# Three Pool transfers instead of one for the first row of a softmax

## The chip, the cores and the metric

The kernel runs on one core of one Trainium2 chip. The metric is the device time of one execution in microseconds (us), of which the profile's span, from the first to the last instruction, is all but about 2 us. A ratio of two kernels is the mean time of the one's fast runs over that of the other's in the same rounds on the same chip, so it is not quite the ratio of the medians quoted beside it; its 95% interval is given in brackets.

## The reference

```python
x = np.random.randn(32, 512, 1024).astype(np.float32); temperature = 0.5

def reference(x, temperature):
    scaled = x / temperature
    shifted = scaled - np.max(scaled, axis=-1, keepdims=True)
    exp_x = np.exp(shifted)
    return (exp_x / np.sum(exp_x, axis=-1, keepdims=True)).astype(np.float32)
```

That is a softmax over 16,384 rows of 1,024 numbers. Each byte is read once and written once: 67 MB in and 67 MB out.

## The kernel before

The rows are taken in 16 passes. A pass is a tile of 128 partitions by 8 rows (4 MB). SyncE loads it, VectorE takes maxima, ScalarE the exponentials with their sums, VectorE divides in place, and ScalarE issues the store. There are six tile buffers, so the seventh load waits for the stores of the first tile. Passes 0, 1, 14 and 15 are worked in two halves of four rows.

```python
ROWS = 8
BUFS = 6
PASSES = [[4, 4]] * 2 + [[8]] * 12 + [[4, 4]] * 2
...
    def load():
        i = len(tiles)
        if i < len(PASSES):
            xt = data.tile([P, ROWS, d], f32, name="xt")
            nc.sync.dma_start(out=xt, in_=dram(xf, i))
            tiles.append(xt)
...
    def store(g):
        i, a, k = groups[g]
        if g == 0:
            nc.gpsimd.dma_start(out=dram(of, i)[:, :1, :], in_=tiles[i][:, :1, :])
        elif a + k == ROWS:
            a = 1 if i == 0 else 0
            nc.scalar.dma_start(out=dram(of, i)[:, a:, :], in_=tiles[i][:, a:, :])
            load()
```

Only the very first row of each partition (128 x 4 KB, 0.5 MB) is stored by Pool, early, while ScalarE is still at work on the second half of the tile.

## Time and profile before

| | before |
|---|---|
| time, median of 6 runs | 317.71 us (317.35 to 317.98) |
| VectorE, ScalarE busy | 79%, 47% of the span |
| loads, ScalarE's stores | 49.7% and 48.9% of the 16 DMA engines |
| Pool's store | 0.4% of the 16 DMA engines |

The lines of the page stand in the prediction below: q1 are the loads, q10 ScalarE's stores, q0 Pool's store and q14 the fetching of instructions. The prediction also says how the trace's packets are strung into 16 chains, one for each DMA engine; "refill engines" are the two whose chains hold the q14 packets. In the kernel before, every chain comes out with exactly 128 load packets, 120 + 8 store packets and, but for one packet swapped between two chains, 8 packets of Pool's row, which is a check on the stringing. "A chain ends at 314.49" below always means this.

### The profile page before, as it was taken

The numbers are of one execution on the slowest core, as the hardware profiler recorded it, in microseconds if no ns is written. First come the engines' busy times: TensorE is split into PE (matmuls) and PEld (weight loads), VectorE is DVE, ScalarE is ACT, GpSimd is POOL, SyncE is SP. The second block draws the span as 40 slices with busy tenths as digits, with TensorE's granted clock in tenths as the row PEclk, the third lists the DMA queues.
The fourth block names the chain that finished last, engine by engine and source line by source line (L and its number), as shares of the span: only waits on it lengthen the run. The fifth ranks groups of instructions, "written<-read, shape, count | busy, mean of one in ns | idle before, by whom it ended". The sixth has DMA issues, their size and how long they took to land. (4 is left out here: it accounts for less than half of the span.)

```text
span 315.7 us, 534 instructions
## 1 busy us (share of the span) xinstructions
DVE 251.0 (79%) x146; ACT 148.1 (47%) x257; POOL 1.3 (0%) x5
## 2 busy tenths in 40 slices
DVE  0399999999679795897949979399793999979710
ACT  0176637680906519074290833808247091564700
POOL 0001000000000000000000000000000000000000
DMA  8999999999999999999999999999999999999996
GB/s 328 415 448 421 369 441 434 465 400 461 404 457 407 457 411 457 428 436 436 428 448 415 448 415 449 411 465 403 461 403 461 403 461 403 461 403 461 407 457 274
DMA packets 4755, 134.24 MB, mean 425 GB/s; under 512 B 528, under 2 KB 528, under 8 KB 656
## 3 DMA queue, kind: packets, MB, share of 16 engines
q1 hardware_dynamic: 2304, 67.11, 49.7%
q10 hardware_dynamic: 2304, 66.59, 48.9%
q0 software_dynamic: 144, 0.52, 0.4%
q14 instruction: 3, 0.02, 0.0%
HBM read 67.11 MB, written 67.11 MB: 425 GB/s over the span
## 5 line engine op out<-in xcount | busy, mean ns | idle before, releaser
L77 ACT ACTIVATE xt<-xt,bias 128x1024 f32<-128x1024 f32 x128 | 145.2, 1135 | 136.6 <-DVE bias L71 127.1
L68 DVE TENSOR_REDUCE top<-xt 128x8 f32<-128x8192 f32 (+1 forms) x20 | 139.5, 6976 | 44.4 <-DMA xt<-in_x_dram 44.4
L95 DVE TENSOR_SCALAR xt<-xt,recip 128x1024 f32<-128x1024 f32 x80 | 54.3, 748 | 0.5
L92 DVE TENSOR_TENSOR xt<-xt,recip 128x8192 f32<-128x8192 f32 x6 | 52.2, 8692 | 0.2
L77 ACT ACTIVATION_READ_ACCUMULATOR xt<-xt,bias 128x1 f32 x128 | 23.9, 187 | 0.0
L77 ACT ACT_TABLE_LOAD x1 | 1.3, 1283 | 13.3 <-DMA xt<-in_x_dram 13.3
L89 DVE RECIPROCAL recip<-sums 128x8 f32<-128x8 f32 (+1 forms) x20 | 3.8, 188 | 4.1 <-ACT xt L77 4.1
L71 DVE TENSOR_SCALAR bias<-top 128x8 f32<-128x8 f32 (+1 forms) x20 | 3.4, 171 | 0.7
L104 POOL DMA_DIRECT2D out_dram<-xt x1 | 1.1, 1142 | 23.4 <-DVE xt L95 23.4
L143 POOL MEMSET const-bfloat16-1.0<- 128x1 bf16 x1 | 0.1, 96 | 0.0
L143 POOL MEMSET const-float32-0.0<- 128x1 f32 x1 | 0.1, 93 | 0.2 <-issue 0.2
L143 POOL MEMSET const-float32-1.0<- 128x1 f32 x1 | 0.1, 93 | 0.0
L143 POOL MEMSET const-uint8-127<- 128x1 uint8 x1 | 0.1, 93 | 0.0
## 6 DMA issues: line engine op xcount, KB each, us to landing
xt<-in_x_dram SPq DMA_DIRECT2D x16, 4096.0 KB, 51.2
out_dram<-xt ACTq DMA_DIRECT2D x15, 4096.0 KB, 28.0
out_dram<-xt ACTq DMA_DIRECT2D x1, 3584.0 KB, 23.2
out_dram<-xt POOLq DMA_DIRECT2D x1, 512.0 KB, 19.6
```

The costliest lines, as they stand in the source:

```text
L68: nc.vector.tensor_reduce(out=top, in_=tiles[i][:, a : a + k, :], axis=mybir.AxisListType.X, op=extreme)
L71: nc.vector.tensor_scalar_mul(bias, in0=top, scalar1=-scale)
L77: nc.scalar.activation(tiles[i][:, a + b, :], tiles[i][:, a + b, :], mybir.ActivationFunctionType.Exp, bias=bias[:, b : b + 1], scale=scal ...
L89: nc.vector.reciprocal(recip, sums)
L92: nc.vector.tensor_mul(xt, xt, recip.unsqueeze(2).to_broadcast([P, k, d]))
L95: nc.vector.tensor_scalar_mul(tiles[i][:, a + b, :], in0=tiles[i][:, a + b, :], scalar1=recip[:, b : b + 1])
L104: nc.gpsimd.dma_start(out=dram(of, i)[:, :1, :], in_=tiles[i][:, :1, :])
L143: nc = _bacc.Bacc("TRN2", target_bir_lowering=False, num_devices=1)
```

## The change

Pool's row is still stored from all 128 partitions, but in parts of 4, 108 and 16.

```diff
+PARTS = (0, 4, 112, 128)
...
         if g == 0:
-            nc.gpsimd.dma_start(out=dram(of, i)[:, :1, :], in_=tiles[i][:, :1, :])
+
+            for p, q in zip(PARTS, PARTS[1:]):
+                nc.gpsimd.dma_start(out=dram(of, i)[p:q, :1, :], in_=tiles[i][p:q, :1, :])
```

## The prediction

What the sum needs is this assumption: the first transfer gives one row to each of 4 engines, the second 9 to each of the other 12, the third one to each of all 16. Then four engines carry 1 + 1 = 2 rows and twelve 9 + 1 = 10, where all had 8. The sum came to 317.8 - 0.5 = 317.3 us, or 317.4 with the rivals; its term of 0.5 us rests on these shares. The shares of the second rival (9, 8 and 4 rows) were assumed as well. The numbers of engines (0 to 15), here and in the expectations, follow the order in which the author took the transfers to fill the engines; no view names an engine.

> **What bounds the kernel now.** I read the page first (parts 1 and 2), then its DMA queues and issues, then the waits of the load queue, and last the DMA view of a short stretch at the end.
>
> ```profile
> DVE 251.0 (79%) x146; ACT 148.1 (47%) x257; POOL 1.3 (0%) x5
> ...
> DMA  8999999999999999999999999999999999999996
> ...
> q1 hardware_dynamic: 2304, 67.11, 49.7%
> q10 hardware_dynamic: 2304, 66.59, 48.9%
> q0 software_dynamic: 144, 0.52, 0.4%
> q14 instruction: 3, 0.02, 0.0%
> ...
> L104 POOL DMA_DIRECT2D out_dram<-xt x1 | 1.1, 1142 | 23.4 <-DVE xt L95 23.4
> ...
> xt<-in_x_dram SPq DMA_DIRECT2D x16, 4096.0 KB, 51.2
> out_dram<-xt ACTq DMA_DIRECT2D x15, 4096.0 KB, 28.0
> out_dram<-xt ACTq DMA_DIRECT2D x1, 3584.0 KB, 23.2
> out_dram<-xt POOLq DMA_DIRECT2D x1, 512.0 KB, 19.6
> ```
>
> No compute engine is near full: VectorE has 79%. The DMA row is 9 in every slice but the first and the last, and the loads (q1) and ScalarE's stores (q10) hold 98.6% of 16 engines' span. So the kernel is bound by the 16 DMA engines: 134 MB in 315.7 us. The changed transfer is queue q0: 0.4% of the DMA time. That alone caps what the change can do in a steady way at about 0.4% of 315.7 us, 1.3 us, unless it creates a wait.
>
> Could it create one? The sixth buffer's successor, the seventh load, reuses the first tile, so it must wait for that tile's stores.
>
> ```profile
> SPq L59 <- DMA out_dram<-xt: 214.3, 10, 42.9
> ```
>
> The load queue waits for stores all the time and it costs nothing, because loads already issued keep the engines fed. In the timeline Pool issues at 23.8 us, so its transfer lands at 23.8 + 19.6 = 43.4; ScalarE's store of the same tile issues at 32.9 and lands at 32.9 + 23.2 = 56.1. The seventh load is released by the second one, 12.7 us after Pool's.
>
> The trace keeps a start, a queue, a size and a duration for each DMA packet. Each starts within some nanoseconds of the end of another, so they string into 16 chains, one for each DMA engine. A 32,768-byte packet takes 1.213 us, a 28,672-byte one 1.062, a 4,096-byte one of Pool's store 0.159. One engine's share is 248 of the first (300.8), 8 of the second (8.5) and 8 of the third (1.3): 310.6 us, and the chains run without a gap worth naming from 1.8 us to 313.2 or later. The span ends 1.2 us after the last chain. So what ends the kernel is not the mean engine but the last one, and the DMA view of 311.8 to 313.8 us, in slices of 0.05 us, shows that they don't end together (each packet stands in the slice in which it starts):
>
> ```profile
> DMA  0009999909900090000000900000090000000000
> GB/s 0 0 0 655 2621 1966 1311 655 0 1311 655 0 0 0 655 0 0 0 0 0 0 0 655 0 0 0 0 0 0 656 0 0 0 0 0 0 0 0 0 0
> ```
>
> 655 GB/s in one slice is one 32 KB packet. Fourteen engines start their last data packet between 311.95 and 312.55; two stragglers start theirs at 312.9 and 313.28, and end at 314.12 and 314.49, when the mean of the other fourteen ends is 313.40 and the latest 313.73. Following these two chains back, they are the ones with the three instruction packets of q14: one has the packet at 84.5 us (0.31 us, and the load packet behind it 0.53 longer than usual: 0.84), the other the two at 65.2 and 190.4 (0.31 + 0.25 and 0.31 + 0.34: 1.2). So the two engines that refill instructions end last, by about what the refills cost, and the worst is 0.76 us behind the latest of the others.
>
> [...] the first packet of Pool's store comes at 28.1 us, 3.1 us after its 1.14 us instruction ended[...].
>
> **The change part by part.** The instruction order against before is the same on every engine but for two more transfers on Pool; the seventh load waits for three Pool completions where it waited for one. Bytes are equal: 128 packets of 4 KB.
>
> *Moved, the packets.* [...] So four engines gain 6 x 0.159 = 0.95 us and twelve lose 2 x 0.159 = 0.32 us. The odd cut (4, 108, 16) makes sense only as this: it frees the engines that refill instructions.
>
> If both stragglers are among the four, they end at 314.49 - 0.95 = 313.54 and 313.17, and the bound becomes the latest of the twelve: between 313.40 + 0.32 = 313.72 (a mean one) and 313.73 + 0.32 = 314.05. The end moves by 314.49 - 314.05 = 0.44 up to 0.77 us earlier; I take 0.5. That is 0.16% of the span.
>
> *Added, on Pool.* Two more issues of about 1.1 us each (estimate from the 1142 ns row, which was for 128 rows; Pool is idle otherwise): free. The last transfer is written out some 2 to 3 us later, and engines with 10 packets need two more rounds of about 1.4 us (a 1.213 us packet of another queue between two of Pool's). So Pool's store lands near 43.4 + 3 + 3 = 49, still before 56.1: no new wait.
>
> *Added, on the load queue.* Two waits before the seventh load, both long satisfied; the gaps on that queue are hidden.
>
> *Completion packets.* 16 of 9 ns for each transfer, so 2 x 9 = 0.018 us per engine. Nothing.
>
> Sum: 317.8 - 0.5 = 317.3 us if the mapping is the intended one. Allowing for the rivals, I say 317.4.
>
> **The rivals.** *The stragglers are not among the four engines.* No view names the DMA engine of a packet, so the trace cannot say which engine refills. Then the last chain gets two more packets and ends 0.32 us later: about 318.1. For it: nothing but ignorance. Against it: the shape of the cut. One in five.
>
> [...]108 partitions as 7 each on fifteen engines and 3 on the last, and 4 and 16 as one each. Then the loads are 9 packets on engines 0 to 3, 8 on the middle ones, 4 on the last. Stragglers among the first four end 0.16 us later, otherwise nothing changes: 317.8 to 318.0. [...] One in five.
>
> *A wait appears*: [...]the completion comes after 56.1 us and holds back the seventh load. Even then the queue of loads issued at the start is not empty (the longest load takes 85.6 us from issue to landing, so it lands well past 85), leaving some 30 us before an engine would run dry. It would take a transfer put on one single engine (108 x 0.159 = 17 us on one chain, or 335 us) to be seen. [...] Two in a hundred.
>
> *The hidden case*: the tail shifts but other jitter (the few long packets at 35 to 37 us, 0.4 to 0.5 us each) gives back the gain: same time as before.
>
> **Range and chances.** The runs of before spread over 0.4 us (317.6 to 317.98). Intended mapping 317.0 to 317.5; rivals 317.8 to 318.2; another 0.3 us for the scatter of the runs. So 316.9 to 318.2. Two per cent is 6.4 us, more than five times the whole transfer's DMA share: faster by that is excluded (0.5%), slower needs the single-engine case (1.5%).
>
> **What would show it right or wrong.** Right: 128 packets of 4 KB still, on chains with 2 and with 10 of them; 48 completion packets on q0; the two refill chains no longer last in the stretch after 311.8 us; the DMA row all 9. The landing of ScalarE's first store still after Pool's. Wrong: a refill chain that ends later than 314.49 with 8 or more Pool packets (mapping), a DMA slice below 9 in the middle (a wait), or instruction packets at other places or more of them, since the program has grown by two instructions. A changed number of refills would move the end by 0.6 to 0.8 us each, more than the change itself.

## The result

The changed kernel took 317.57 us (median of 6 runs, 317.39 to 318.53), the kernel before 317.71; the ratio is 1.000 [0.9987, 1.0014]. In a second comparison on another occasion (run e12_after below) it was 317.48 against 317.46, ratio 0.9999 [0.9987, 1.0011]. The time is the same. The predicted 317.4 with its range of 316.9 to 318.2 holds it, but the gain of 0.4 that the figure stood for isn't there, and the profile shows why.

These are the lines of the page of the changed kernel that answer to those shown of before (queue or group, packets or count, then megabytes and shares, or busy time):

```profile
DVE 251.1 (79%) x146; ACT 148.2 (47%) x257; POOL 2.5 (1%) x7
...
DMA  8999999999999999999999999999999999999996
...
q1 hardware_dynamic: 2304, 67.11, 49.7%
q10 hardware_dynamic: 2304, 66.59, 48.8%
q0 software_dynamic: 192, 0.52, 0.4%
q14 instruction: 3, 0.02, 0.0%
...
L108 POOL DMA_DIRECT2D out_dram<-xt x3 | 2.3, 776 | 23.2 <-DVE xt L97 23.2
...
out_dram<-xt ACTq DMA_DIRECT2D x1, 3584.0 KB, 23.4
out_dram<-xt POOLq DMA_DIRECT2D x1, 432.0 KB, 20.8
out_dram<-xt POOLq DMA_DIRECT2D x1, 64.0 KB, 24.9
out_dram<-xt POOLq DMA_DIRECT2D x1, 16.0 KB, 7.5
```

Nothing moved but q0, and there one number matters: 192 packets, where it had 144. Pool's row is still 128 packets of 4 KB. So there are 64 small ones. Pool's one transfer of before left 16 completion packets (144 - 128), so three make 48. Sixteen are left over. In the record of q0 they are of 4 bytes and 9 ns like the completions, and they stand where an engine has no row to move: the first transfer (4 rows) has one on each of the twelve engines without a row, and the second has four on a single engine. 12 + 4 = 16. I call them padding.

That gives away how the 108 partitions were split: not 9 on each of 12 engines, but 7 on each of 16, rounded up, with the last engine filled up by four padding packets (15 x 7 + 3 = 108). The chains agree, but for a packet or two that neighbours exchange in the stringing: four engines carry 9 rows, eleven carry 8 and one carries 4. The two engines that refill instructions are among the four with 9. They were to be freed of six rows and got one more.

The DMA view of 311.8 to 313.8 us of the changed kernel, in slices of 0.05 us, is the answer to the one in the prediction:

```profile
DMA  0099099999900000090000900000000900000000
GB/s 0 0 655 655 0 655 2621 1311 1311 655 655 0 0 0 0 0 0 655 0 0 0 0 655 0 0 0 0 0 0 0 0 656 0 0 0 0 0 0 0 0
```

The last packet now starts in the 32nd slice (313.35 us), where it started in the 30th (313.25). The chains of the two refill engines end at 314.61 and 314.13; before they ended at 314.49 and 314.12. One row is 0.159 us, and 0.12 is not far from it, but single traces of kernels with equal shares differ by more (314.16 to 314.49 below), so this difference is not to be leaned on.

The wait of the load queue is what it was (waiter, what it waited for, us in total, times, longest):

```profile
SPq L61 <- DMA out_dram<-xt: 223.9, 11, 46.6
```

Pool's three transfers landed by 50.3 us (the last one issued at about 25.4 and took 24.9), and ScalarE's store of the same tile at 32.7 + 23.4 = 56.1. The seventh load was issued at 56.1 us, where it was at 56.2.

### The profile page after: what moved, and what is told of

Same layout as the page of the kernel before. It is cut to its first block, busy times and chain, and to the rows that moved or that the text cites. A ratio compares the mean times of both kernels' runs of the same rounds, so it can differ in the third digit from the quotient of the medians.

```text
span 315.9 us, 540 instructions
## 1 busy us (share of the span) xinstructions
DVE 251.1 (79%) x146; ACT 148.2 (47%) x257; POOL 2.5 (1%) x7
## 5 line engine op out<-in xcount | busy, mean ns | idle before, releaser
L108 POOL DMA_DIRECT2D out_dram<-xt x3 | 2.3, 776 | 23.2 <-DVE xt L97 23.2
## 6 DMA issues: line engine op xcount, KB each, us to landing
out_dram<-xt ACTq DMA_DIRECT2D x1, 3584.0 KB, 23.4
out_dram<-xt POOLq DMA_DIRECT2D x1, 64.0 KB, 24.9
```

What stands on the lines that cost most here:

```text
L108: nc.gpsimd.dma_start(out=dram(of, i)[p:q, :1, :], in_=tiles[i][p:q, :1, :])
```

## The experiments

There are two theories to part. **Mapping**: the relief would have worked, but the 108 partitions were laid over all 16 engines, 7 on each of fifteen and 3 on the last, so it never took place. **No worth**: even with the intended shares the tail would not come earlier. A lever was needed that changes the shares with everything else alike. What I tried, on a guess, is whether the shares depend on the number of dimensions that a transfer counts along: writing each row as two pieces adds a second dimension, and the packets then tell what the shares are.

### e1: the intended shares

```diff
-                nc.gpsimd.dma_start(out=dram(of, i)[p:q, :1, :], in_=tiles[i][p:q, :1, :])
+                nc.gpsimd.dma_start(
+                    out=dram(of, i)[p:q, :1, :], in_=tiles[i][p:q, :1, :], max_dma_last_dim=2048
+                )
```

> Edit: the same three transfers of 4, 108 and 16 partitions, but each 4 KB row is written as two pieces of 2 KB, so that a transfer counts along a second dimension. Theory (padding): a transfer that counts along partitions alone is laid over all 16 engines[...] rounded up, and padded with 4-byte packets; the trace of the changed kernel shows it, 64 four-byte packets on q0 where three transfers over 16 engines need 48. [...] Then 48 four-byte packets on q0, four engines with 2 rows and twelve with 10, the two refill engines in the group with 2 rows; last chain between 313.6 and 314.1 us instead of 314.61, time 0.4 to 0.8 us below the kernel before. Rival (the mapping does not matter, the tail is set by something else): tail and time as before, within 0.2 us. Rival (the refill engines are in the other group): last chain 314.8, time 0.3 us above.

Measured: 318.75 us (318.01 to 321.17) against 317.30; ratio 1.0052 [1.0024, 1.008]. The shares came out as intended: 48 four-byte packets, and 48 of eight bytes that are padding (12 engines x 1 row for the first transfer, 4 x 9 for the second); four chains with 2 rows and twelve with 10; both refill engines among the four. They end at 313.83 and 313.84, that is 0.66 and 0.28 earlier than before. And yet the kernel is 0.5% slower, where I had expected 0.4 to 0.8 us less. The DMA view of 312 to 315.2 us (slices of 0.08 us, 410 GB/s is one 32 KB packet) shows the tail:

```profile
DMA  0909099900990900909099000090000000090000
GB/s 0 819 0 410 0 410 2048 1229 0 0 410 819 0 410 0 0 819 0 410 0 410 410 0 0 0 0 410 0 0 0 0 0 0 0 0 410 0 0 0 0
```

The cluster of fourteen engines has dissolved. Last packets start all the way from 312 to 314.8, and the last chain ends at 316.08. The mean of the sixteen ends moved from 313.48 to 314.32, although the bytes are the same. Part of this is plain: load packets took longer, by 2.08 us on an average engine over the run where before it was 1.56 (over 1.213 us a packet), so 0.52 of the 0.84. Another 0.22 is idleness between 300 and 310 us: some engines ran out of work because the last store was issued late. The rows of the timeline with that issue, in the kernel before, the changed one and e1 (start, duration, what):

```profile
300.97 0.34 ACTq L107 DMA_DIRECT2D out_dram<-xt  x1
```

```profile
301.68 0.34 ACTq L111 DMA_DIRECT2D out_dram<-xt  x1
```

```profile
303.14 0.34 ACTq L113 DMA_DIRECT2D out_dram<-xt  x1
```

A tile is worked on only when its slowest engine has landed it: in the kernel before, each of the ten times that VectorE waited for a load, it began 0.36 to 0.37 us after the last of the load's 16 completion packets. For the last load the first and the last engine are 1.5 us apart before, 2.4 in the changed kernel and 5.0 in e1. So both theories of the start were too simple: the mapping did decide the shares, but with the intended shares other engines end later.

### e2: the control for the pieces

```diff
-            nc.gpsimd.dma_start(out=dram(of, i)[:, :1, :], in_=tiles[i][:, :1, :])
+            nc.gpsimd.dma_start(
+                out=dram(of, i)[:, :1, :], in_=tiles[i][:, :1, :], max_dma_last_dim=2048
+            )
```

> Control for the run above: one transfer of 128 partitions as in the kernel before, but with its rows written as two pieces of 2 KB. Every engine gets 8 rows. Expected from every theory: 16 four-byte packets on q0, stragglers at about 314.5 us, time within 0.2 us of the kernel before; if the 2 KB pieces alone cost something, it shows here as the same amount on every engine (16 packets of 2 KB against 8 of 4 KB).

Measured: 317.50 us against 317.30; ratio 1.0007 [0.9995, 1.0019]. 16 four-byte packets, 8 rows on each engine, refill engines at 314.23 and 313.96. The rows travel in packets of 4 KB as before, two pieces in one packet, not in 16 of 2 KB as I had written. The pieces cost nothing that these runs can tell.

### e3 and e4: many small transfers, with and without the second dimension

e3, from the changed kernel (and ScalarE's first store then starts at row 4):

```diff
-PARTS = (0, 4, 112, 128)
+PARTS = tuple(range(0, 32, 4)) + (32, 128)
-                nc.gpsimd.dma_start(out=dram(of, i)[p:q, :1, :], in_=tiles[i][p:q, :1, :])
+                nc.gpsimd.dma_start(out=dram(of, i)[p:q, :4, :], in_=tiles[i][p:q, :4, :])
-            a = 1 if i == 0 else 0
+            a = 4 if i == 0 else 0
```

> Edit: Pool stores all four rows of the first group (16 KB for each partition), as eight transfers of 4 partitions and one of 96; ScalarE's first store covers the other four rows. The effect is four times as large as with one row. Theory[...]: each of the eight small transfers puts its four rows on the same four engines, which then carry 8 + 6 = 14 rows where the others carry 6: 6 rows of about 0.61 us above the mean of 8, so the refill engines end about 3.6 us later, 321.4 us (1.1% slower), with 16 x 9 + 8 x 12 = 240 four-byte packets on q0. Rival[...]: 2 + 6 = 8 rows on every engine, 144 four-byte packets, time as before within 0.3 us.

e4 is e3 with `max_dma_last_dim=8192` in Pool's transfer.

> Edit: as the run above, but each 16 KB row is written as two pieces of 8 KB, which adds a second counting dimension. Theory[...]: the eight small transfers go to engines 0 to 3, 4 to 7, 8 to 11 and 12 to 15 twice, so every engine carries 8 rows, 144 four-byte packets on q0, and the time is within 0.4 us of the kernel before. Rival (many small Pool transfers are slow by themselves, through their issue or their completions): as slow as the run above, about 321 us.

In these expectations a row of 16 KB is put at 0.61 us, an estimate: half of the 1.213 us of a 32 KB packet.

Measured, e3: 327.57 us against 317.30, ratio 1.0316 [1.0291, 1.0341]; e4: 323.22, ratio 1.0184 [1.0148, 1.0221]. The counts are those of the theory to the packet: e3 has 240 four-byte packets on q0, with 14 rows on four chains and 6 on twelve; e4 has 16 packets of 8 KB, which is 8 rows, on every chain, and 336 four-byte packets (144 completions, and 8 transfers x 12 engines x 2 pieces of padding; I had left the padding out of my 144). So the mapping is shown from both sides.

The times are both far above what I expected, so here the size was wrong, and the page of e4 says why (out<-in, issuer, count, KB, us to landing):

```profile
out_dram<-xt ACTq DMA_DIRECT2D x1, 2048.0 KB, 20.2
out_dram<-xt POOLq DMA_DIRECT2D x1, 1536.0 KB, 72.2
```

Pool's last transfer was issued at 33.3 us and landed 72.2 us later, at 105.5. That is long after ScalarE's store of the same tile (32.9 + 20.2 = 53.1). The seventh load was issued at 78.5 us instead of 56.2; in e3 and e4 it takes the second tile's buffer, and ScalarE's store of that tile landed at 78.4 in e4. The eighth, into the first tile's buffer, was issued at 105.5 instead of 75.9, when Pool's store landed. This is the third rival of the prediction, a Pool store that comes to hold the loads back, made real by four times the bytes. e3 and e4 thus settle the mapping, but their times mix it with this wait and the other order of the buffers, and can't be used for the size of anything.

### e5: without the cut at 4

```diff
-PARTS = (0, 4, 112, 128)
+PARTS = (0, 112, 128)
```

> Edit: the changed kernel without its cut at 4: two transfers, of 112 and 16 partitions, rows whole. Theory (padding rule): 112 partitions are 7 for each of 16 engines without padding, 16 are one each, so 8 rows everywhere and 32 four-byte packets on q0; ends and time as the kernel before within 0.2 us; the two refill engines last at 314.1 and 314.5. Rival (the number of Pool transfers matters): some tenths of a us above before.

Measured: 317.55 us against 317.46; ratio 0.9998 [0.9986, 1.0010]. 32 four-byte packets and no padding, 8 rows everywhere; the refill engines end at 314.12 and 314.16. So the cut at 4 is what makes the shares of the changed kernel uneven, and the time doesn't notice either form.

### e12: the changed kernel again

No edit: the changed kernel, in the same rounds as e5, e10 and e11.

> The changed kernel itself, beside the kernel before in the same rounds as the other three. Theory (its four engines carry 9 rows, not 2): refill engines among those with 9 rows, last chain 314.6, time 0 to 0.3 us above before. Rival (the relief works as intended): 0.4 us or more below before.

Measured: 317.48 against 317.46, ratio 0.9999 [0.9987, 1.0011]. The packets are as in the first trace (192 on q0, 64 of them of four bytes); the two refill engines end at 314.50 and 314.13 (undoing one exchange of chains, which shows as 129 load packets on one and 127 on the other) and everybody else by 313.86. The first theory holds.

### e6 and e7: what makes the two late engines late

e6 treats two rows of 1,024 as one of 2,048, so its result is wrong. The essential lines:

```diff
-ROWS = 8
+ROWS = 4
-PASSES = [[4, 4]] * 2 + [[8]] * 12 + [[4, 4]] * 2
+PASSES = [[2, 2]] * 2 + [[4]] * 12 + [[2, 2]] * 2
-    xf = x.flatten_outer_dims()
+    xf = x.flatten_outer_dims().rearrange("(n two) d -> n (two d)", two=2)
```

> Edit to the kernel before, wrong result on purpose: two rows of 1024 are treated as one row of 2048, so ScalarE and VectorE have about half the instructions for the same elements; all transfers are as before (Pool still one of 128 x 4 KB). Theory (the two late DMA engines are late because they fetch instructions): the three instruction packets after the start fall to none or one, the two stragglers disappear, and the last chain ends near 313.7 us instead of 314.49, so the time falls by 0.5 to 0.9 us. Rival (they are late for another reason, the instruction packets only happen to be there): stragglers at 314.1 and 314.5 as before, time within 0.2 us.

e7 adds instructions to ScalarE and leaves the result right:

```diff
                 accum_out=sums[:, b : b + 1],
             )
+            for _ in range(3 if 3 <= i <= 9 else 0):
+                nc.scalar.activation(dummy, dummy, mybir.ActivationFunctionType.Exp, scale=-1.0)
```

> Edit to the kernel before: three one-element exponentials of a scratch tile after each exponential of passes 3 to 9, 168 more ScalarE instructions, result unchanged. Theory (instruction packets make the straggler): one or two more instruction packets on the DMA engine that already has two, each 0.55 to 0.85 us, last chain 315.0 to 315.9, time 0.5 to 1.4 us above before. Rival (instruction packets don't set the end): same time within 0.2 us, since ScalarE has room (47% busy).

e7: 318.88 us against 317.28, ratio 1.0053 [1.0040, 1.0066]. The page and the DMA view of 312 to 316.2 us (slices of 0.105 us):

```profile
q14 instruction: 5, 0.04, 0.0%
```

```profile
DMA  9907707007070000000000070000000000000000
```

Five instruction packets where there were three, and the lonely packet of the tail starts at 314.4. Four of the five are on one chain, at 65.1, 114.1, 172.8 and 271.5 us; it ends at 315.66, 1.17 us later than the last chain before. The fifth, at 84.8, is alone on another chain, which ends at 314.19. So the chain with two packets is the one that fetches ScalarE's instructions, two more packets cost it 1.17 us, and that reaches the time in full (the spans of the two profiles differ by 1.24 us, the medians by 1.6, a little more than the 1.4 expected at most). ScalarE at 56% is no bound. The theory holds.

e6: 317.05 against 317.28 in the medians, but two of six runs at 318.6 and 318.8, ratio 1.0007 [0.9988, 1.0026]: inconclusive as a time. In its trace the instruction packets fell to two, one on each of two chains, not to one or none. These end at 313.65 and 313.94, and a third chain that had no refill ends last, at 314.04. The tail got 0.45 us shorter than before, less than I expected, since ordinary stragglers stand close behind.

### e8, e9, e10, e11: other shares, with each row in two pieces

All four are e1 with other cuts, so the diff is the line of `PARTS`:

```diff
-PARTS = (0, 4, 112, 128)
+PARTS = (0, 4, 16, 128)               # e8
+PARTS = (0, 4, 64, 128)               # e9
+PARTS = (0, 4, 40, 44, 80, 128)       # e10
+PARTS = (0, 2, 77, 80, 125, 128)      # e11
```

> Edit: three transfers as in the first experiment (2 KB pieces[...]), but cut at 4 and 16: 4 rows on engines 0 to 3, 12 on 4 to 15, 112 on all 16 as 7 each, so every engine carries 8 rows. It has the number of transfers, the pieces and the rule of the first experiment without its unevenness. Theory (uneven shares did the harm there: the twelve engines with ten rows drift away from the four with two, each tile lands with the slowest, and load packets become longer): same time as before within 0.3 us, no long load packets after 60 us but those behind instruction packets. Rival (three transfers[...]): 1 us or more above before, as the first experiment.

> Edit: as the run above but cut at 4 and 64: 4 rows on engines 0 to 3, 60 on engines 4 to 15 as 5 each, 64 on all as 4 each: 5 rows on the four engines, 9 on the twelve, so half the shift of the first experiment. Theory (two effects: the refill engines gain 3 x 0.159 = 0.48 us, the twelve lose 0.16 and drift): refill engines end 0.3 to 0.5 us earlier; if drift grows with the shift the time lies between the even cut and the first experiment, 0 to +0.7 us; if a small shift brings no drift, the hoped-for gain shows, -0.3 us. Rival (as the first rival above): +1 us whatever the cut.

> Edit: five transfers[...] (2 KB pieces), cut at 4, 40, 44 and 80: 4 rows on engines 0 to 3, 36 on engines 4 to 15, the same again, 48 on all: 5 rows on the four engines, 9 on the twelve. This is the half of the first experiment's shift that the cut at 64 missed[...]. Theory (relief and drift): refill engines end 0.48 us earlier than with the even cut; if drift needs a large shift, time 0.2 to 0.5 us below before; if it grows in step with the shift, 0 to +0.7 us, with long load packets after 60 us beyond those behind instruction packets.

> Edit: five transfers[...], cut at 2, 77, 80 and 125: 2 rows on engines 0 and 1, 75 on fifteen engines from 2 on (skipping 1), 3 on engines 1 to 3, 45 on fifteen from 4 on (skipping 3), 3 on engines 3 to 5. In sum 5 rows on engine 1, 7 on engine 3, 9 on engines 0, 2, 4 and 5, 8 on the ten others. The cut at 64 showed that one refill engine (one instruction packet) is number 3; that the other (two packets) is number 1 is a guess, it is one of 0 to 2. Theory: if the guess is right, the last chain ends between 313.9 and 314.1 instead of 314.5, without drift, since only two engines are relieved and nobody gets more than one row; time 0.3 to 0.6 us below before. If it is engine 0 or 2: it has 9 rows, last chain 314.6, time 0.1 above.

e8 (8 rows on each engine): 317.24 against 317.28, ratio 0.9997 [0.9985, 1.0009]. So three transfers with their rows in two pieces are not what harms e1. What is left is its uneven shares, or what comes with them.

e9: 317.50 against 317.28, ratio 1.0006 [0.9994, 1.0018]. My expectation had the shares wrong. q0 has 12 + 4 packets of eight bytes, and the engine with the four has 5 rows, the others 8 or 9: so the second transfer put 4 rows on each of fifteen engines and left out only one of the first transfer's four (number 3 in the expectation of e11). This turned out useful. The engine with four padding packets and 5 rows is the one with the single instruction packet, and it ends at 313.56, where it ends at 313.92 to 314.16 with 8 rows (e2, e5, e8, before). Three rows are 3 x 0.159 = 0.48 us. So the relief works on the engine that gets it. ScalarE's refill engine has 9 rows here and ends last, at 314.47, and the time stays.

e10 (5 rows on four engines, 9 on twelve): 319.88 (317.95 to 320.71) against 317.46, ratio 1.0064 [1.0036, 1.0091], where at most 0.7 us was expected. Half the shift of e1 costs no less than all of it; the intervals overlap. The trace is of one of its longer runs (320.67). Its refill engines end at 314.40 and 314.38, with the bulk, and other engines at 315.3 to 317.7. As in e1 the last store comes late (303.8 us) and engines idle before it, 0.67 us on average.

e11 was meant as the version that beats both: relief for the two refill engines alone, one more row at most for four others. It took 318.12 against 317.46, ratio 1.0017 [1.0005, 1.0029], a little slower. The guess was right: the chain with 5 rows is ScalarE's refill engine, which ends at 313.89. The other one ends at 314.44 by the stringing that fits the gaps best, at 313.22 by the next best; neither ends last. Two chains without any refill end at 315.35 and 314.87. They lost 2.0 and 1.6 us to packets that ran longer than usual after 45 us: 0.94 and 1.00 of it to loads, the rest to store packets of Pool and ScalarE.

### All shares side by side

Rows of Pool's store on ScalarE's refill engine / on the other refill engine / on the rest; where those two chains and the latest of the rest end; load packets between 90 and 300 us that took over 40 ns longer than usual (one of them stands behind the instruction packet at 190 to 194 us in each of these kernels); the distance between the first and the last engine in landing the last load. The chains, not a view of the profile, are the source.

```
kernel   rows       refill engines   latest other  long loads  landing  ratio
before   8/8/8      314.49  314.12   313.73         1          1.5 us   1
e5       8/8/8      314.12  314.16   313.46         6          2.1      0.9998
e8       8/8/8      314.14  313.92   314.15         1          1.1      0.9997
e2       8/8/8      314.23  313.96   313.82         8          1.8      1.0007
e9       9/5/8-9    314.47  313.56   313.74         1          1.4      1.0006
after    9/9/4-9    314.61  314.13   313.90         1          2.4      1.000
e11      5/7/8-9    313.89  314.44   315.35        12          2.3      1.0017
e10      5/5/5-9    314.40  314.38   317.69        27          5.0      1.0064
e1       2/2/2-10   313.83  313.84   316.08        35          5.0      1.0052
```

The three kernels in which another engine ends 0.9 us or more behind both refill engines (e11, e10, e1) are the three with most long load packets, and the three that are slower. In e1 and e10 the engines also land a tile 5 us apart. Uneven shares alone don't do it: the changed kernel has 4 to 9 rows, e9 5 to 9, and each has one long load.

**What stays open** is what makes a packet longer. In e1 the long ones (by up to 0.43 us each) come about once in a pass (some 19 us) and mostly begin with, or 2.4 us after, the packet that completes a store on their engine. The same moments pass without harm in the kernel before. Whether the engines keep in step doesn't part the kernels, at least by a coarse count: how many of a tile's eight loads an engine has done when a store completes on it. The number of engines that agree on it is 16 in e8 and e10, 13 in the changed kernel and e11, 9 in e2 and e1, and of each pair only the second is harmed. And e11 has 12 long packets with a landing distance of 2.3 us. Two things mark e1, e10 and e11: Pool's store ends later (52.9 to 56.6 us on q0, against 43 to 50 in the others of this table), and the seventh load goes out later (57.1, 58.1 and 57.3 us, against 54.8 to 56.5). It waited for ScalarE's store of the first tile, in e11 for Pool's last transfer, by 0.1 us. These two, the shares and the ending of stores are bound together in these runs, and no run parts them.

## Why the prediction was right or wrong

- **The bound, and that no wait appears.** Right: the DMA row is 9 in both kernels but for the first and the last slice, and the seventh load went out at 56.1 us. The prediction put the landing of Pool's store at 49; it was 50.3. Pool's two more issues cost 1.2 us of its idle time, not the 2.2 estimated, since the smaller transfers took less (2.31 us for three, 1.14 for one). The first packet came 3.1 us after the first of them, about as before (3.2; the prediction read 3.1); what makes this delay no run tests.
- **The two refill engines end last, by what the refills cost.** Right, and shown by e7: two more instruction packets, 1.17 us later. In the kernel before, a refill took 0.31 us for its packet of 8 KB and made the load packet behind it 0.25 to 0.53 us longer.
- **"Moved, the packets": 4 + 12 engines, then all.** This is the step that failed: the relief of six rows for each refill engine, from which the gain of 0.5 us followed. The prediction assumed 2 and 10 rows and gave its rival of 9, 8 and 4 rows one chance in five; the rival came, so the refill engines got one row more. The rival's 0.16 us on the last chain can't be told from nothing: 0.12 in one trace and 0.01 in the other. "48 completion packets" was right as to completions, but q0 shows 64, since the padding was not thought of.
- **"Moved": the bound becomes the latest of the twelve, 313.72 to 314.05.** This also fails, though only e1 could show it. Given the intended shares, the refill engines did leave the tail, but the latest of the twelve ended at 316.08. (The lower figure started from 313.40 as the mean of the other fourteen ends; redone from the trace it is 313.36, which changes nothing.) The sum took 0.32 us for two rows as the whole cost of an engine and treated the 16 chains as independent. They aren't: a tile waits for its slowest engine, the last store was issued 2.2 us later, and load packets became longer by 0.52 us on the mean engine.
- **The range and the chances.** The range held, and the rival that came true was in it. That the point 317.4 fits so well is luck: it was pulled down by a gain that did not exist, and the gain was no larger than the scatter of the runs. The measured change of the medians is 0.14 us down in one comparison and 0.02 up in the other.
- **"Straggler relief" as an aim.** The mechanism is real for a single engine (e9: 0.4 to 0.6 us for three rows). None of the versions tried turned it into time.

## What to carry to other kernels

When a kernel is bound by its DMA engines, look at the engines one by one: a change of a transfer's shape that looks idle can change how many of its packets an engine gets. Here the cuts at 4 and 112 gave the refill engines 9 rows with whole rows (the changed kernel) and 2 with each row in two pieces (e1). The packet counts of the queue, padding included, show it at once: 192 on q0 in the one, 224 in the other. Before trusting a rebalancing, make the shares come out as meant and see whether the other engines stay as fast as they were: here the version that gave twelve engines a quarter more of a 0.4% transfer took 0.5% longer.
